# Grouped-query attention: V blocks loaded in two halves, other loads moved, and one set of Q transposes put later

## The chip, the core and the metric

The kernel runs on one core of a Trainium2 chip. A core has five engines that work side by side, each through its own list of instructions in order: TensorE (PE; matmuls, and a part for weight loads, PEld), VectorE (DVE), ScalarE (ACT), GpSimd (POOL) and SyncE (SP). Sixteen DMA engines move data between device memory and the core's SBUF. A DMA is issued by an engine's list, here SP's, POOL's or ACT's, and runs by itself from then on; an issue on POOL takes POOL's time. Matmuls write to PSUM, which PE, DVE and ACT reach.

The metric is the time on the device of one execution, in microseconds (us). It is the median of several executions; one more execution was recorded by the profiler.

## The reference

Q is (8, 512, 32, 64): batch, sequence, heads, dimension. K and V have 8 heads, each shared by four heads of Q. All are float32.

```python
scale = 1.0 / np.sqrt(dim)
scores = np.einsum('bhqd,bhkd->bhqk', Q, K_expanded) * scale
weights = np.exp(scores - np.max(scores, axis=-1, keepdims=True))
weights = weights / (np.sum(weights, axis=-1, keepdims=True) + 1e-10)
output = np.einsum('bhqk,bhkd->bhqd', weights, V_expanded)
return output.transpose(0, 2, 1, 3).astype(np.float32)
```

## The kernel before, in words

**Blocks, units and jobs.** The eight batch entries are the blocks 0 to 7. The work is cut into 64 jobs; a job `j` is one K/V head of one block with its four Q heads (two pairs), so block `b` has jobs 8b to 8b+7, and two jobs make a unit `u`. A job computes sixteen 128 x 512 pieces of scores (two pairs, four quarters of the keys, two heads), takes their exponentials, multiplies by V (with a column of ones behind V, so that the sums of the weights come out of the same products), and divides. No maximum is subtracted; `check_sums` and `check_v` gather evidence that this was safe, and a general path behind the fast one would run if it wasn't.

**Two ways to an exponential.** Most of a job's scores go two pieces at a time through ACT (`act_tile`, line 300; seven tiles in a job, numbered 0 to 6). Two or three pieces of each job go another way: DVE turns the scores into an integer `u` (`exp_d`, line 317), takes low bits `f` of it (line 334), POOL makes `g` of `f` (line 339) and `w` of `g` and `f` (line 345), and DVE adds `u` and `w` into the weights `pt` (`exp_d4`, line 358). The sum for job j is made in the loop step of job j+1, just ahead of job j+1's own `f`. So the chain goes round from POOL to DVE to POOL: `w` of one job, sum, `f`, `g`, `w` of the next.

**Kinds of jobs.** With `WIDE` and `ALONE` (lines 41 to 44) there are three: wide jobs give three pieces to DVE and POOL; narrow jobs (2, 8, 14, 20, ... 62) give two; and the wide job just ahead of a narrow one (7, 13, 19, 25, ...), called lone job here, has its `g` made by DVE instead of POOL, behind the first step of its last normalisation. Six jobs, from a narrow one to the next, make a round.

**The order of the work** is written out by hand: the loop at line 574 issues, for each job, the loads listed for it in `LOADS`, the K transposes listed in `KEYS`, the scores of this job, the products of the job before (`pv`, line 386, on PE), the normalisation of the job before (`norm`, lines 418 and 425, on DVE) and the transposes of a Q that will be used two jobs later (`trans_q`: eight transposes on PE, line 219, into a bank of PSUM, and one copy out by DVE, line 224). Waits between engines are put in by the language's bookkeeping of who wrote and read which tile. Where that bookkeeping would order two instructions that touch different banks of one tile, the kernel takes the order out by hand with `apart`, which tells it so; `trans_q` has an argument `other` for that.

**Loads.** All loads of Q, K and V in the loop are issued by POOL, at the head of the job's step, that is behind the `w` of the job before and ahead of the job's own `g`. `load_q` brings half a block of Q, `load_k` and `load_v` a block of K or V. V is held in two buffers, `vt[b % 2]`, four quarters of 128 keys each; V's block b overwrites block b-2, so it waits for the last product with that one, which is in the step of job 8(b-1). V rows lie 65 elements apart (the column of ones between), so a load of V writes 128 x 32 separate runs of 64 elements; a load of K writes 128 long runs, a load of Q 512. `check_v` (line 242) reads one quarter of a V block in each of four jobs listed in `CHECKS`; `check_sums` (line 399, three reductions) comes in the jobs of `SUMS`: 14, 20, 26, 38, 44, 50 and 62, narrow jobs all.

**K** is transposed by DMAs on SP's list (`dma_k`), which also stores the results; three result buffers are in turn.

**The start.** The first three jobs run by a branch of their own (`if j < 3`). In job 2 two sets of Q transposes are made instead of one, for jobs 3 and 4, into the two banks of one PSUM tile, one behind the other, between ACT tiles 3 and 4; Q for job 4 is loaded in job 1.

Of the kernel before, what the change touches and what calls it, by code (L numbers as in the profile page):

```python
# [70 lines left out]
def fast_path(ctx, tc, Q, K, V, out, flag, ident):  # L71
    nc = tc.nc
    B, S, H, D = Q.shape
    KV = K.shape[2]
    HPG = H // KV
    SC = S // 128
# [31 lines left out]
    vt = [const_pool.tile([128, SC, KV, D + 1], BF16, name=f"v{j}") for j in range(2)]  # L108
# [14 lines left out]

    def load_v(b, lo=0):
        to = vt[b % 2][:, :, lo:, 0:D]
        of = V[b, :, lo:, :].rearrange("(p sc) g d -> p sc g d", p=128)
        if lo:
            for sc in range(SC):
                nc.gpsimd.dma_start(out=to[:, sc], in_=of[:, sc])  # L129
        else:  # L130
            nc.gpsimd.dma_start(  # L131
                out=to.rearrange("p sc g d -> p (sc g) d"),
                in_=of.rearrange("p sc g d -> p (sc g) d"),
            )

# [15 lines left out]
    def d_tile():  # L151
        return d_pool.tile([128, 2, S], FP32, name="d_ps")
# [113 lines left out]
    SUMS = dict(zip((14, 20, 26, 38, 44, 50, 62), range(B - 1)))  # L266
    KEYS = dict(zip((4, 10, 17, 28, 33, 41, 52), range(1, B)))

    def in_jobs(load, first, jobs):
        for n, j in enumerate(jobs):  # L270
            LOADS.setdefault(j, []).append((load, first + n))

    LOADS = {1: [(load_q, 1, 0, 2 * HPG), (load_q, 1, 2 * HPG, 4 * HPG)]}
    in_jobs(load_k, 1, [3, 8, 15, 22, 30, 39, 46])
    in_jobs(load_q, 2, [3, 5, 9, 12, 16, 21, 23, 28, 33, 35, 40, 45, 47, 52])
    in_jobs(load_v, 1, [7, 13, 19, 25, 37, 43, 49])

# [16 lines left out]
    def act_tile(j, n):  # L294
        group = act_tiles(j)[n]
        i, kc, lo = group[0]
        ps = s_tile()
        for _, _, m in group:
            scores(j, ps[:, m, :], i, kc, m)
        return nc.scalar.activation(  # L300
            out=jobs[j]["pt"][:, i, kc, lo:, :], in_=ps[:, lo:, :], func=EXP, scale=scale
        )
# [203 lines left out]
    load_v_head(0, 1)  # L506
    load_v(0, 2)
    nc.gpsimd.memset(ones, 1.0)
# [65 lines left out]
    for j in range(1, NJOB - 1):  # L574
# [12 lines left out]
        def transposes(bank, beside=None):  # L587
            ahead = (j + 1,) if j < 2 else (3, 4) if j == 2 else (j + 2,)
            return [
                trans_q(to, bank[:, n, :], other=beside)[1]  # L590
                for n, to in enumerate(ahead) if to < NJOB
            ]

# [7 lines left out]
        if j < 3:  # L601
# [25 lines left out]
        elif taken(j) < 3:  # L627
# [8 lines left out]
            act_tile(j, 4)  # L636
            reads = transposes(d_tile()) if j + 2 < NJOB else []
            exp_d4(last)
            for read in reads:
                read()  # L640
# [8 lines left out]
        elif not ALONE(j):  # L649
# [15 lines left out]
            if after:  # L665
                act_tile(j, 6)
            reads = transposes(bank, beside)
            if not after:
                act_tile(j, 6)
            exp_d4(last)  # L670
            exp_d2(j)
            for read in reads:
                read()
            pv(last, 1, cut, 32)
            norm(last, 1)
        else:
# [11 lines left out]
            act_tile(j, 5)  # L688
            reads = transposes(bank, beside)
# [4 lines left out]
            for read in reads:  # L694
                read()
            open_job(j + 1)
# [149 lines left out]
```

## Time and profile before

| | |
|---|---|
| median of three executions | 406.32 us (405.81 to 406.45) |
| profiled execution, its own time | 405.98 us |
| its span, first to last instruction | 404.2 us |
| granted TensorE clock | 0.999 |
| ACT busy | 394.1 us, 97% |
| DVE busy | 369.6 us, 91% |
| PE busy | 362.4 us, 90% |
| POOL busy | 294.8 us, 73% |
| whole V loads in the loop, issue on POOL | 7 of 1765 ns |

A page of the profile gives busy times by engine and by group of instructions (line, engine, operation, what is written from what, shapes, count, busy us, mean ns, idle time before them and what ended it). Behind it the trace can be asked for the instructions of one engine in order of time, and for the busy time of every engine in chosen stretches of the span. A long busy share doesn't say that an engine is the bound in every stretch; what an engine waited for, and when, does. Instructions on ACT and DVE overlap a little where one follows the other at once, so the mean duration of an ACT tile (1118 ns) is longer than the step from one to the next.

### The profile page before, as it was taken

The numbers are of one execution on the slowest core, as the hardware profiler recorded it, in microseconds if no ns is written. First come the engines' busy times: TensorE is split into PE (matmuls) and PEld (weight loads), VectorE is DVE, ScalarE is ACT, GpSimd is POOL, SyncE is SP. The second block draws the span as 40 slices with busy tenths as digits, with TensorE's granted clock in tenths as the row PEclk, the third lists the DMA queues.
The fourth block names the chain that finished last, engine by engine and source line by source line (L and its number), as shares of the span: only waits on it lengthen the run. The fifth ranks groups of instructions, "written<-read, shape, count | busy, mean of one in ns | idle before, by whom it ended". The sixth has DMA issues, their size and how long they took to land.

```text
span 404.2 us, 13018 instructions
## 1 busy us (share of the span) xinstructions
PE 362.4 (90%) x5670; PEld 223.9 (55%) x5670; DVE 369.6 (91%) x645; ACT 394.1 (97%) x454; POOL 294.8 (73%) x173
## 2 busy tenths in 40 slices
PE   7999889998998998899999989988999899899885
PEld 3555556555554655555555555555555555555554
DVE  4779999999999999999989899999999999898896
ACT  6999999999999999999999999999999999999995
POOL 9848787696786687777767786876887676756853
PEclk9999999999999999999999999999999999999999
DMA  9999899989697997989719798699895968222216
GB/s 148 144 198 198 183 255 216 153 186 193 150 216 189 172 206 155 157 158 186 234 66 181 126 291 160 102 203 185 205 208 164 137 108 227 108 106 105 76 40 205
DMA packets 82893, 67.73 MB, mean 168 GB/s; under 512 B 52752, under 2 KB 57872, under 8 KB 82832
## 3 DMA queue, kind: packets, MB, share of 16 engines
q0 software_dynamic: 45072, 24.91, 49.2%
q1 hardware_dynamic: 36688, 41.49, 35.0%
q8 instruction: 45, 0.74, 0.8%
q10 hardware_dynamic: 1072, 0.46, 0.4%
q14 instruction: 16, 0.13, 0.1%
HBM read 50.33 MB, written 33.55 MB: 208 GB/s over the span
## 4 chain that ended last, share of the span: by engine, by line
POOL 28%; PE 27%; DVE 20%; ACT 19%; issue 3%; DMA 2%; ACTq 0%; POOLq 0%; DVEq 0%
ACT pt L300 19%; POOL w L345 17%; PE pv L386 13%; PE s_ps L282 10%; POOL g L339 8%; DVE pt L358 8%; DVE f L334 5%; PE d_ps L219 3%; DVE o_sb L425 3%; DMA q_nat<-in_Q_dram 2%; DVE u L317 2%; DVE qt L224 1%; POOL v L129 1%; DVE inv L418 1%; DVE g L339 1%
## 5 line engine op out<-in xcount | busy, mean ns | idle before, releaser
L300 ACT ACTIVATE pt<-s_ps 128x1024 f16<-128x1024 f32 x397 | 377.3, 1118 | 2.0 <-PE s_ps L282 0.7
L345 POOL TENSOR_TENSOR w<-g,f 128x1536 bf16<-128x1536 bf16 (+1 forms) x63 | 182.3, 2894 | 25.6 <-DVE g L339 21.3
L386 PEld LDWEIGHTS <-pt 128*128 128x128 f16 x4096 | 140.5, 98 | 69.2 <-DVE o_sb L425 35.6
L386 PE MATMUL pv<-v,pt 128*128 128x65 bf16 x4032 | 170.1, 195 | 7.1 <-DVE o_sb L425 5.5
L282 PE MATMUL s_ps<-qt,kt 64*128 64x512 bf16 x742 | 145.1, 384 | 21.1 <-ACT pt L300 17.7
L339 POOL TENSOR_SCALAR g<-f 128x1536 bf16<-128x1536 int16 (+1 forms) x52 | 71.1, 1368 | 76.3 <-DVE f L334 60.1
L317 DVE TENSOR_SCALAR u<-d_ps 128x1024 int16<-128x1024 f32 (+1 forms) x114 | 111.9, 981 | 2.1 <-PE d_ps L282 1.8
L282 PEld LDWEIGHTS <-kt 64*128 64x128 bf16 x960 | 50.0, 93 | 88.0 <-issue 62.2
L425 DVE TENSOR_TENSOR o_sb<-pv,inv 128x512 f32<-128x512 f32 x112 | 77.3, 691 | 3.7 <-DVE inv L418 0.2
L358 DVE TENSOR_TENSOR pt<-u,w 128x1536 uint16<-128x1536 int16 (+1 forms) x64 | 57.4, 897 | 3.1
L282 PE MATMUL d_ps<-qt,kt 64*128 64x512 bf16 x218 | 42.1, 377 | 4.9 <-DVE qt L224 4.3
L224 DVE COPY qt<-d_ps 128x1024 bf16<-128x1024 bf16 x62 | 42.4, 685 | 0.3
L219 PE MATMUL d_ps<-ident,q_nat 128*128 128x128 bf16 x496 | 38.2, 220 | 0.4 <-DMA q_nat<-in_Q_dram 0.4
L334 DVE TENSOR_SCALAR f<-u 128x1536 int16<-128x1536 int16 (+1 forms) x64 | 37.6, 588 | 0.0
L310 ACT ACTIVATE pt<-d_ps 128x512 f16<-128x512 f32 x50 | 35.0, 701 | 0.0
L418 DVE RECIPROCAL inv<-pv 128x8 f32<-128x8 f32 x112 | 22.7, 203 | 12.3 <-PE pv L386 11.9
L219 PEld LDWEIGHTS <-q_nat 128*128 128x128 bf16 x508 | 29.0, 98 | 8.2 <-issue 7.5
L242 DVE TENSOR_REDUCE okv<-v 128x1 f32<-128x512 bf16 x32 | 21.6, 675 | 0.0
L146 POOL DMA_DIRECT2D q_nat<-in_Q_dram x19 | 15.5, 817 | 0.1
L282 PE MATMUL s_ps<-qt,kt_first 64*128 64x512 bf16 x54 | 10.3, 382 | 2.5 <-ACT pt L300 1.8
L131 POOL DMA_DIRECT2D v<-in_V_dram x7 | 12.4, 1765 | 0.0
L425 DVE TENSOR_TENSOR o_sb<-pv,inv_last 128x512 f32<-128x512 f32 x14 | 9.7, 691 | 0.4
(61 smaller groups left out, 60.5 us busy)
## 6 DMA issues: line engine op xcount, KB each, us to landing
out_dram<-o_sb SPq DMA_DIRECT2D x31, 1024.0 KB, 5.9
q_nat<-in_Q_dram POOLq DMA_DIRECT2D x14, 1024.0 KB, 10.5
k_nat<-in_K_dram POOLq DMA_DIRECT2D x7, 512.0 KB, 5.3
kt<-kt SPq DMA_DIRECT2D x14, 256.0 KB, 5.4
v<-in_V_dram POOLq DMA_DIRECT2D x7, 512.0 KB, 8.3
q_nat<-in_Q_dram POOLq DMA_DIRECT2D x3, 512.0 KB, 7.9
out_dram<-o_sb SPq DMA_DIRECT2D x3, 256.0 KB, 2.4
kt<-k_nat SPq DMA_TRANSPOSE x32, 6.3
```

The costliest lines, as they stand in the source:

```text
L219: nc.tensor.transpose(ps[:, i, sc, :], qn[u // 2][:, sc, h:h + 2, :], ident),
L224: return done, lambda: apart(nc.vector.tensor_copy(out=qt[u][:, g, lo:hi, :], in_=ps[:, lo:hi, :, :].rearrange("p i sc c -> p i (sc c)")), ...
L282: return nc.tensor.matmul(ps, keys[64 * m:64 * m + 64, g if u == 0 else g ^ m, kc * 128:(kc + 1) * 128], qt[u][64 * m:64 * m + 64, g, i, : ...
L300: return nc.scalar.activation(out=jobs[j]["pt"][:, i, kc, lo:, :], in_=ps[:, lo:, :], func=EXP, scale=scale)
L310: left = nc.scalar.activation(out=st["pt"][:, i, kc, m:, :], in_=ps[:, m:, :], func=EXP, scale=scale)
L317: return nc.vector.tensor_scalar(out=out, in0=in_, scalar1=A_U, scalar2=B_U, op0=ALU.mult, op1=ALU.add)
L334: nc.vector.tensor_single_scalar(out=st["f"], in_=st["u"], scalar=1023, op=ALU.bitwise_and)
L339: (nc.vector if odd else engine).tensor_scalar(out=st["g"], in0=st["f"], scalar1=-EXP_F1, scalar2=EXP_K * 2.0 ** (24 * by_bits), op0=ALU.a ...
L345: engine.tensor_tensor(out=st["w"], in0=st["g"], in1=st["f"].bitcast(FP16) if by_bits else st["f"], op=ALU.mult,)
L358: nc.vector.tensor_tensor(out=st["pt"][:, DPAIR, :, :, :].rearrange("p kc m q -> p (kc m) q")[:, d_block(j):d_block(j) + n, :].bitcast(U16 ...
L386: nc.tensor.matmul(st["pv"][i][:, m, qc, :], st["pt"][:, i, kc, m, qc * 128:(qc + 1) * 128], vt[b % 2][:, kc, 2 * gp + g, :], start=(n < 2 ...
L425: nc.vector.tensor_tensor(out=osb[u][:, :, h:h + 2, :].rearrange("p qc m d -> p m qc d"), in0=sums[:, :, :, 0:D], in1=inv[:, :, :, None].t ...
```

## The change

**V.** `load_v` takes two of the four quarters at a time. Block 1 is still loaded whole, in job 7. Blocks 2 to 7 come in two issues each, in jobs 9 and 14, 20 and 21, 26 and 27, 33 and 38, 44 and 45, 50 and 51: narrow jobs or the ones behind these. Before, they came whole in jobs 13, 19, 25, 37, 43 and 49, which are lone jobs. The opening's V load is the same four issues under another name.

**Other loads.** Q loads move from jobs 9, 21, 33 and 45 to 10, 22, 34 and 46, K loads from 22 and 46 to 24 and 48. The K transposes of block 5 on SP move from job 33 to job 35.

**Job 2.** The second set of Q transposes, for job 4, and its copy go behind ACT tile 4 and the first eleven products of the second pair. The rest of the edits turn lists of one into single values.

```diff
-    def load_v(b, lo=0):
-        to = vt[b % 2][:, :, lo:, 0:D]
-        of = V[b, :, lo:, :].rearrange("(p sc) g d -> p sc g d", p=128)
-        if lo:
-            for sc in range(SC):
-                nc.gpsimd.dma_start(out=to[:, sc], in_=of[:, sc])
-        else:
-            nc.gpsimd.dma_start(
-                out=to.rearrange("p sc g d -> p (sc g) d"),
-                in_=of.rearrange("p sc g d -> p (sc g) d"),
-            )
+    def load_v(b, lo=0, hi=SC):
+        nc.gpsimd.dma_start(
+            out=vt[b % 2][:, lo:hi, :, 0:D].rearrange("p sc g d -> p (sc g) d"),
+            in_=V[b].rearrange("(p sc) g d -> p sc g d", p=128)[:, lo:hi].rearrange(
+                "p sc g d -> p (sc g) d"
+            ),
+        )
+
+    def first_v(lo):
+        of = V[0, :, lo:, :].rearrange("(p sc) g d -> p sc g d", p=128)
+        for sc in range(SC):
+            nc.gpsimd.dma_start(out=vt[0][:, sc, lo:, 0:D], in_=of[:, sc])
...
-    KEYS = dict(zip((4, 10, 17, 28, 33, 41, 52), range(1, B)))
+    KEYS = dict(zip((4, 10, 17, 28, 35, 41, 52), range(1, B)))
...
-    in_jobs(load_k, 1, [3, 8, 15, 22, 30, 39, 46])
-    in_jobs(load_q, 2, [3, 5, 9, 12, 16, 21, 23, 28, 33, 35, 40, 45, 47, 52])
-    in_jobs(load_v, 1, [7, 13, 19, 25, 37, 43, 49])
+    in_jobs(load_k, 1, [3, 8, 15, 24, 30, 39, 48])
+    in_jobs(load_q, 2, [3, 5, 10, 12, 16, 22, 23, 28, 34, 35, 40, 46, 47, 52])
+    in_jobs(load_v, 1, [7])
+    for b, at in enumerate(((9, 14), (20, 21), (26, 27), (33, 38), (44, 45), (50, 51)), 2):
+        for n, j in enumerate(at):
+            LOADS.setdefault(j, []).append((load_v, b, n * SC // 2, (n + 1) * SC // 2))
...
-    load_v(0, 2)
+    first_v(2)
...
         def transposes(bank, beside=None):
-            ahead = (j + 1,) if j < 2 else (3, 4) if j == 2 else (j + 2,)
-            return [
-                trans_q(to, bank[:, n, :], other=beside)[1]
-                for n, to in enumerate(ahead) if to < NJOB
-            ]
+            return trans_q(j + (1 if j < 3 else 2), bank[:, 0, :], other=beside)[1]
...
             bank = d_tile()
-            reads = transposes(bank)
-            if j == 1:
-                reads.append(first_k(1, 1, bank[:, 1, :])[1])
+            read = transposes(bank)
+            beside = first_k(1, 1, bank[:, 1, :])[1] if j == 1 else None
             exp_d4(last)
             exp_d2(j)
-            for read in reads:
-                read()
+            read()
+            if beside:
+                beside()
             act_tile(j, 4)
             pv(last, 1, 0, 11)
+            if j == 2:
+                trans_q(4, bank[:, 1, :])[1]()
             act_tile(j, 5)
...
```

More of the change, by code (lines that the diff above doesn't have):

```diff
@@ L636, in fast_path @@
             act_tile(j, 4)
-            reads = transposes(d_tile()) if j + 2 < NJOB else []
+            read = transposes(d_tile()) if j + 2 < NJOB else None
             exp_d4(last)
-            for read in reads:
+            if read:
                 read()
@@ L666, in fast_path @@
                 act_tile(j, 6)
-            reads = transposes(bank, beside)
+            read = transposes(bank, beside)
             if not after:
@@ L671, in fast_path @@
             exp_d2(j)
-            for read in reads:
-                read()
+            read()
             pv(last, 1, cut, 32)
@@ L688, in fast_path @@
             act_tile(j, 5)
-            reads = transposes(bank, beside)
+            read = transposes(bank, beside)
             act_tile(j, 6)
@@ L693, in fast_path @@
             rest = exp_d2(j)
-            for read in reads:
-                read()
+            read()
             open_job(j + 1)
```

## The prediction

> **What bounds the kernel now.** I read the page's first parts, then stretches of the span cut at the starts of narrow jobs, then the order of instructions on single engines. The page first:
>
> ```profile
> span 404.2 us, 13018 instructions
> PE 362.4 (90%) x5670; PEld 223.9 (55%) x5670; DVE 369.6 (91%) x645; ACT 394.1 (97%) x454; POOL 294.8 (73%) x173
> ```
>
> ACT is 97% busy, so a gain can only be time in which ACT runs late. Busy stretches of six jobs, each from the first exp of a narrow job to that of the next, show where (columns: stretch, us, then busy us and instructions of PE, weight loads, DVE, ACT, POOL; clock; DMA). The clock is 1.00 in all:
>
> ```profile
> 55.85:92.32 36.47, 33.57 (x534) 20.64 (x530) 34.59 (x59) 36.47 (x43) 28.31 (x15) 1.00 1.03 176
> 129.08:165.82 36.74, 33.40 (x534) 20.65 (x530) 35.47 (x62) 36.60 (x44) 28.27 (x15) 1.00 0.97 199
> 165.82:202.57 36.75, 33.40 (x534) 20.64 (x530) 35.46 (x63) 36.61 (x43) 25.83 (x13) 1.00 0.94 173
> 202.57:238.91 36.34, 33.33 (x533) 20.75 (x530) 32.03 (x54) 36.34 (x43) 27.73 (x14) 1.00 0.77 168
> 349.78:386.12 36.34, 33.31 (x533) 20.73 (x530) 31.98 (x55) 36.34 (x44) 24.53 (x11) 1.00 0.24 89
> ```
>
> The two stretches of 36.34 us are those whose lone job just ahead (31, 55) issues no V load. Two with V loads take 36.74 and 36.75, the first 36.47; the other V stretches are like these two or longer. The narrow jobs alone (14 to 20 and so on; here 20, 32, 62 and 8):
>
> ```profile
> 129.08:135.93 6.85, 5.89 (x96) 3.65 (x93) 6.78 (x16) 6.71 (x8) 3.20 (x2) 1.00 1.65 212
> 202.57:208.90 6.33, 5.96 (x96) 3.76 (x93) 5.66 (x12) 6.33 (x8) 3.28 (x2) 1.00 0.00 0
> 386.12:392.45 6.33, 5.55 (x89) 3.40 (x86) 6.13 (x15) 6.33 (x9) 3.45 (x2) 1.00 0.01 3
> 55.85:62.38 6.53, 6.07 (x96) 3.65 (x93) 5.91 (x13) 6.53 (x8) 3.75 (x3) 1.00 1.46 111
> ```
>
> Job 20 has a V load ahead and the three reductions of `check_sums` (16 DVE instructions): 6.85. Job 62 has the reductions and no V load: 6.33, as job 32 with neither. Job 8 has a V load and no reductions: 6.53. So V is needed for the loss, and the loss is 0.52 us where both meet. What V does there, on POOL and DVE around jobs 13 to 16, and DVE in job 31, which has no V load (instructions in order of time: start us, us, engine, line, operation; in brackets the idle time before it and what ended it):
>
> ```profile
> 90.54 1.77 POOL L131 DMA_DIRECT2D v<-in_V_dram  x1
> 93.90 3.08 POOL L345 TENSOR_TENSOR w<-g,f 128x1536 bf16<-128x1536 bf16 x1 [1.58 <-DVE g L339]
> 102.27 0.62 POOL L118 DMA_DIRECT2D k_nat<-in_K_dram  x1
> ...
> 90.63 0.96 DVE L358 TENSOR_TENSOR pt<-u,w 128x1536 uint16<-128x1536 int16 x1
> 91.50 1.17 DVE L334 TENSOR_SCALAR f<-u 128x1536 int16<-128x1536 int16 x1
> 98.49 0.42 DVE L334 TENSOR_SCALAR f<-u 128x1024 int16<-128x1024 int16 x1
> 103.46 0.55 DVE L334 TENSOR_SCALAR f<-u 128x1536 int16<-128x1536 int16 x1
> 106.57 0.67 DVE L242 TENSOR_REDUCE okv<-v 128x1 f32<-128x512 bf16 x1
> ...
> 200.88 0.96 DVE L358 TENSOR_TENSOR pt<-u,w 128x1536 uint16<-128x1536 int16 x1
> 201.76 0.56 DVE L334 TENSOR_SCALAR f<-u 128x1536 int16<-128x1536 int16 x1
> ```
>
> The V issue occupies POOL for 1.77 us (90.54 to 92.31). The DVE step `f` that begins at 91.50 beside it takes 1.17 us instead of 0.55 or 0.56: its work ran from 92.12 (92.67 less 0.55), 0.19 us before the issue's recorded end. The sum `pt<-u,w` beside the same issue is not slowed (0.96 both times). So `f` waits while POOL issues, and `g`, `w` and the next narrow job come 0.61 us late.
>
> **The change, part by part.** *V halves.* A half writes half the runs of 64 elements: 128 x 16 = 2048. Issue times per load, by runs: 4096 for a whole V, 768 for the opening's quarter loads, 512 for a full Q, 128 for a full K:
>
> ```profile
> L131 POOL DMA_DIRECT2D v<-in_V_dram x7 | 12.4, 1765 | 0.0
> L129 POOL DMA_DIRECT2D v<-in_V_dram x4 | 3.4, 891 | 0.0
> L146 POOL DMA_DIRECT2D q_nat<-in_Q_dram x19 | 15.5, 817 | 0.1
> L118 POOL DMA_DIRECT2D k_nat<-in_K_dram x9 | 5.8, 644 | 0.0
> ```
>
> A line from 768 to 4096 gives 891 + 1280 x 0.263 ns = 1.23 us, one from 128 gives 1.19; I take 1.2, with ends 0.64 and 1.77. Six whole loads (10.6 us of POOL) become twelve halves (14.4 us). Where they go:
> In narrow job 14 POOL is free from 96.98 (end of `w`), and its next step, `g`, needs `f`, which starts at 98.49 behind the sum and the `qt` copy. A half from 96.9 ends at 98.1: it meets no `f` and holds up no `g`. Cost 0; without that cover, 1.2.
> In the job behind POOL comes to its loads at 102.27 (here K's); a half would run to 103.47, let `f` go at 103.28 by the 0.19 above, and `f` is due at 103.46: cost 0, with 0.18 to spare. At the upper end (1.77) it would let go at 103.85, and `f` would be 0.39 late: 6 x 0.39 = 2.3 us. Jobs 9 and 33 wait also for the last reader of the old V; PE finishes job 7's last products at 61.97 and POOL gets to its load at 65.48:
>
> ```profile
> 61.30 0.67 PE L386 MATMUL pv<-v,pt 128*128 128x65 bf16 x16
> 65.48 0.82 POOL L146 DMA_DIRECT2D q_nat<-in_Q_dram  x1
> 73.54 1.47 POOL L339 TENSOR_SCALAR g<-f 128x1536 bf16<-128x1536 int16 x1 [1.55 <-DVE f L334]
> L131 POOL DMA_DIRECT2D v<-in_V_dram x7: 1762/1762/1771, 53.8 to 311.0; - x7
> DMA to landing us min/median/max: 7.5/8.3/10.7
> ```
>
> That leaves 3.5 us, so nothing queued behind on POOL (`g`, `w`) waits. What is gained: jobs 13, 19, 25, 37, 43 and 49 lose their V load, job 7 keeps it. A plain stretch takes 36.75 (mean of the two shown) against 36.34: 0.41 each (0.52 in the narrow job, 0.11 given back later, since POOL's loop g, w, `pt`, `f` is then next to bind), 6 x 0.41 = 2.46 us. What makes some V stretches longer still I leave as it is.
>
> The Trainium skill, "SBUF — State Buffer", section "Who interferes with whom", says that a DVE instruction in a two-port mode and GpSimd lock each other out for the whole instruction. By it `f` would start only at 92.31, at 1.2 us the job behind would lose 6 x 0.01, and at 1.77 it would lose 6 x 0.58 = 3.5 instead of 2.3; the measured start, 92.12, is kinder, and I go by it.
>
> *Q and K moved.* Four Q loads go one job later, two K loads two jobs: each stands alone in a wide job, where POOL waits 1.55 us for `f` (row at 73.54) and the issue takes 0.82 or 0.64. Cost 0; uncovered, 0.8 each. Nobody needs them for four jobs (24 us at 36.34 / 6 each). The transposes of K block 5 on SP start two jobs later; stores behind them have three buffers. Cost 0. The opening's four V loads are the same.
>
> *Third job.* Rows of PE, ACT and DVE in job 2, and of DVE in job 1:
>
> ```profile
> 20.98 0.62 PE L219 MATMUL d_ps<-ident,q_nat 128*128 128x128 bf16 x8
> 21.96 0.62 PE L219 MATMUL d_ps<-ident,q_nat 128*128 128x128 bf16 x8 [0.36 <-DMA q_nat<-in_Q_dram]
> 22.51 0.39 PE L282 MATMUL s_ps<-qt,kt_first 64*128 64x512 bf16 x2
> ...
> 22.95 6.52 ACT L300 ACTIVATE pt<-s_ps 128x1024 f16<-128x1024 f32 x7 [0.52 <-PE s_ps L282]
> 29.29 0.67 ACT L310 ACTIVATE pt<-d_ps 128x512 f16<-128x512 f32 x1
> ...
> 15.78 0.42 DVE L334 TENSOR_SCALAR f<-u 128x1024 int16<-128x1024 int16 x1
> 16.11 0.69 DVE L224 COPY qt<-d_ps 128x1024 bf16<-128x1024 bf16 x1
> 22.21 0.42 DVE L334 TENSOR_SCALAR f<-u 128x1024 int16<-128x1024 int16 x1
> 22.62 1.29 DVE L224 COPY qt<-d_ps 128x1024 bf16<-128x1024 bf16 x2
> ```
>
> Now PE stands 0.36 us before the second set, whose Q lands at 21.96, and ACT idles 0.52. ACT's step per tile is (29.29 - 22.95) / 7 = 0.91; tiles that follow closely overlap, so about 0.2 more is lost: the fifth tile (number 4 from 0) could begin at 22.23. With the second set moved, the scores of tile 4 run at 21.53 and that 0.72 us is won. But the moved set writes the second half of a two-bank tile after the copy out of its first half has been put into the program. The kernel declares such pairs free of each other wherever it wants them so (`apart`, "the two are in different banks of one tile"), and the new call passes no `other`. So I take it that PE must now wait for the first copy. The rows hint at such whole-tile waits: in job 2 the first copy starts 0.41 after `f`, just when the second set ends (22.58), in job 1 0.33 after. In the new order the copy runs from 22.54 to 23.23, PE transposes from about 23.28 to 23.83 (0.55 to the next start, as 21.96 to 22.51), and the scores of tile 5 end at 24.22, so that ACT has them at 24.27 (0.44 after the PE start, as 22.51 to 22.95). Before, tile 5 began at 22.95 + 0.91 = 23.86. Net loss 0.41, bounds -0.57 (no wait: scores of tile 5 from 22.85, ACT at 23.29) and +0.41. What is queued on PE behind the wait (scores of tiles 5 and 6, the products between, job 3) shifts with it, and ACT, the bound, has nothing to give it back with. The copy of the moved set is needed only in job 4.
>
> The Trainium skill, "PSUM — Partial Sum Buffer", section "PSUM bank collisions raise a hardware error", has accesses of two engines to different banks run clean. By it no wait is needed between the copy and the moved set, and the sum here would be -0.57; no run here shows which the program does.
>
> *Sum.* -2.46 + 0.41 = -2.05 us. The profiled execution took 405.98 us (span 404.2 and 1.8 around it), 0.34 below the median of 406.32, so 403.9 profiled and 404.3 as a median.
>
> **Rivals.** *No wait on the copy.* Speaks for it: two different banks. Against it: the missing declaration. -2.46 - 0.57 gives 403.3.
> *The gain isn't V's.* The two stretches of 36.34 us lack not only V but also the reductions and the checks of V (DVE 32.0 against 35.5 us busy). Were DVE late for those, only job 8's share would come back: 36.47 - 36.34 = 0.13 each, 0.8 in all: 405.9. Against it: job 62. Or the halves take `f` with them in the job behind, at the upper end of their issue: -2.05 + 2.3 gives 406.6.
> *Slower: V lands late for its check.* DVE reads the first quarter of a V block in jobs 22, 28, 46 and 52, two jobs after its half is issued instead of three after the whole. By job 14 (issue from 96.9) and job 16 (check at 106.57) that leaves 9.7 us. A whole V lands in 7.5 to 10.7 us; a half should take less. Were each a microsecond and a half over that, `f` and everything behind DVE's wait would slip four times: 4 x 1.5 - 2.05 = +4.0, 410.3. It outweighs the gain from 9.7 + 2.05/4 = 10.2 us on.
>
> **How the numbers follow.** Forecast 0.60 (its own range 403.5 to 405.0); no wait on the copy 0.13; gain not V's, or lost behind the narrow jobs, 0.16; V late 0.06; small things I don't see 0.05. About 0.2% (0.8 us, so 405.5 to 407.1) is what a measurement here can tell from no change. Faster: 0.60 + 0.13 + 0.05 from the third case + 0.01; same: 0.11 of the third and 0.02; slower: 0.06 and 0.02. The range 402.9 to 405.9 takes in the no-wait case with a margin and the 405.9 of the third.
>
> **What would show it.** Every 1536-wide `f` at 0.55, but job 7's; V issues of 1.2 us, twelve; stretches of 36.3 from job 14 on, narrow jobs at 6.33; in job 2 a PE wait of about a microsecond for DVE's `qt` copy and ACT idle of about 0.9 at tile 5. Wrong if `f` is long in jobs 9, 15 or 21, if DVE waits for V in job 22, or if ACT doesn't stop in job 2.

## The result and the profile after

The changed kernel took 404.48 us (median of 14 executions, 404.03 to 405.72), the kernel before 406.02 us measured beside it. The ratio is 0.9966, with a 95% interval of 0.9957 to 0.9975: 1.0 to 1.7 us faster. One of the 14 executions of the kernel before took 488.24 us and is left out of the ratio. The profiled execution of the changed kernel took 404.53 us at a clock of 0.999. Line numbers move by four: ACT's tiles are now line 304, `f` is 338, `g` 343, `w` 349, the copy `qt` 225.

The first lines of the changed kernel's page:

```profile
span 402.8 us, 13022 instructions
PE 362.8 (90%) x5670; PEld 225.2 (56%) x5670; DVE 366.4 (91%) x645; ACT 392.6 (97%) x454; POOL 298.6 (74%) x179
```

Three of the stretches of six jobs, which answer to those of before (columns as there: stretch, us, busy us and instructions of PE, weight loads, DVE, ACT, POOL; clock; DMA):

```profile
129.67:166.04 36.37, 33.34 (x534) 20.86 (x531) 34.90 (x62) 36.37 (x44) 28.91 (x16) 1.00 0.92 189
166.04:202.41 36.37, 33.36 (x535) 20.85 (x532) 34.90 (x62) 36.37 (x44) 28.16 (x15) 1.00 1.07 182
202.41:238.77 36.36, 33.33 (x534) 20.85 (x531) 32.04 (x55) 36.36 (x43) 27.20 (x14) 1.00 0.79 133
```

The two stretches that took 36.74 and 36.75 us now take 36.37, hardly more than the one that never had a V load ahead of it (36.36). From the start of job 8 to that of job 62 it was 386.12 - 55.85 = 330.27 us before and is 384.65 - 56.88 = 327.77 now: 2.50 us less. Job by job, the six narrow jobs behind the old V loads take 3.03 us less in sum, and the other jobs 0.54 more, of it 0.18 in job 22 alone. The longest stretches, from jobs 38 and 50, went from 37.09 and 37.03 us to 36.57 and 36.64, so they gained as well but did not come to 36.3. Narrow jobs 20 and 8, and job 2:

```profile
129.67:136.04 6.37, 5.99 (x98) 3.88 (x95) 6.24 (x15) 6.37 (x9) 4.46 (x3) 1.00 0.40 128
56.88:63.43 6.55, 6.08 (x96) 3.66 (x93) 5.92 (x13) 6.55 (x9) 3.76 (x3) 1.00 1.52 141
19.25:26.73 7.48, 6.25 (x96) 3.96 (x96) 5.10 (x10) 6.56 (x8) 4.21 (x4) 1.00 1.00 136
```

Job 20 went from 6.85 to 6.37, beside 6.36 and 6.32 for jobs 32 and 62; job 8, behind the one whole load that is left, stays at 6.55. Job 2 takes 7.48 us. V's issue in job 21 on POOL, and on DVE `f` of job 13, which lost its load, and of job 21:

```profile
139.03 1.22 POOL L125 DMA_DIRECT2D v<-in_V_dram  x1
...
92.54 0.55 DVE L338 TENSOR_SCALAR f<-u 128x1536 int16<-128x1536 int16 x1
140.35 0.55 DVE L338 TENSOR_SCALAR f<-u 128x1536 int16<-128x1536 int16 x1
```

The twelve halves take POOL 1.22 to 1.24 us each, and `f` is 0.55 or 0.56 us in every wide job but 7. In job 2, on PE, ACT and DVE:

```profile
23.94 0.61 PE L220 MATMUL d_ps<-ident,q_nat 128*128 128x128 bf16 x8 [0.89 <-DVE qt L225]
...
24.91 5.61 ACT L304 ACTIVATE pt<-s_ps 128x1024 f16<-128x1024 f32 x6 [0.92 <-PE s_ps L286]
...
23.20 0.68 DVE L225 COPY qt<-d_ps 128x1024 bf16<-128x1024 bf16 x1
```

PE stands 0.89 us for DVE's first copy, and ACT stands 0.92 us for the scores behind it. The span shrank by 1.4 us (404.2 to 402.8), though, and not by the forecast's 2.05. The rest is in the opening, which both kernels share. The first exponentials on ACT in the two profiled executions, before and then after:

```profile
5.47 1.09 ACT L546 ACTIVATE pt<-s_ps 128x512 f16<-128x512 f32 x2 [0.59 <-PE s_ps L282]
```

```profile
6.12 1.08 ACT L550 ACTIVATE pt<-s_ps 128x512 f16<-128x512 f32 x2 [0.93 <-PE s_ps L286]
```

ACT begins 0.65 us later. So -2.50 (jobs 8 to 61) + 0.41 (job 2, 7.48 against 7.07) + 0.65 = -1.44.

### The profile page after: what moved, and what is told of

Same layout as the page of the kernel before. It is cut to its first block, busy times and chain, and to the rows that moved or that the text cites. A ratio compares the mean times of both kernels' runs of the same rounds, so it can differ in the third digit from the quotient of the medians.

```text
span 402.8 us, 13022 instructions
## 1 busy us (share of the span) xinstructions
PE 362.8 (90%) x5670; PEld 225.2 (56%) x5670; DVE 366.4 (91%) x645; ACT 392.6 (97%) x454; POOL 298.6 (74%) x179
## 4 chain that ended last, share of the span: by engine, by line
ACT 44%; PE 33%; DVE 11%; POOL 8%; issue 2%; ACTq 0%; DVEq 0%; POOLq 0%
ACT pt L304 42%; PE pv L390 15%; PE s_ps L286 13%; POOL w L349 5%; DVE pt L362 4%; PE d_ps L220 4%; POOL g L343 3%; DVE f L338 2%; ACT pt L314 2%; DVE u L321 2%; DVE o_sb L429 1%; DVE qt L225 1%; PE s_ps L518 1%; DVE inv L422 1%; ACT pt L550 0%
## 5 line engine op out<-in xcount | busy, mean ns | idle before, releaser
L286 PEld LDWEIGHTS <-kt 64*128 64x128 bf16 x960 | 51.1, 93 | 90.4 <-issue 65.1
L314 ACT ACTIVATE pt<-d_ps 128x512 f16<-128x512 f32 x50 | 37.9, 758 | 0.0
L338 DVE TENSOR_SCALAR f<-u 128x1536 int16<-128x1536 int16 (+1 forms) x64 | 33.9, 530 | 0.0
L125 POOL DMA_DIRECT2D v<-in_V_dram x13 | 16.5, 1267 | 0.0
```

The costliest lines, as they stand in the source:

```text
L286: return nc.tensor.matmul(ps, keys[64 * m:64 * m + 64, g if u == 0 else g ^ m, kc * 128:(kc + 1) * 128], qt[u][64 * m:64 * m + 64, g, i, : ...
L314: left = nc.scalar.activation(out=st["pt"][:, i, kc, m:, :], in_=ps[:, m:, :], func=EXP, scale=scale)
L338: nc.vector.tensor_single_scalar(out=st["f"], in_=st["u"], scalar=1023, op=ALU.bitwise_and)
```

## The experiments

Each version was measured beside executions of the kernel before on the same chip, whose median was between 406.06 and 406.27 us. Times are medians; a ratio is to that kernel, with its 95% interval in brackets. Times of versions that ran on different chips compare best by their ratios.

**V and the other loads alone.** Job 2 in its old order:

```diff
         def transposes(bank, beside=None):
-            return trans_q(j + (1 if j < 3 else 2), bank[:, 0, :], other=beside)[1]
+            ahead = (j + 1,) if j < 2 else (3, 4) if j == 2 else (j + 2,)
+            return [
+                trans_q(to, bank[:, n, :], other=beside)[1]
+                for n, to in enumerate(ahead) if to < NJOB
+            ]
...
-            if j == 2:
-                trans_q(4, bank[:, 1, :])[1]()
```

> The changed kernel with the third job's order put back as it was before: V, Q, K and the K transposes alone. Theory (the prediction's sum): the loss of 0.41 us in job 2 goes away and nothing else changes. Job 2 (first ACT tile of job 2 to that of job 3) takes 7.07 us instead of 7.48, the stretches from job 14 on 36.3, the time 0.4 us below the changed kernel's, 404.1. Rival (the set is moved because ACT gives the 0.41 back later, or the opening's first loads matter more): the time is the changed kernel's within 0.2 us.

404.13 us (403.52 to 405.34), ratio 0.9955 (0.9942 to 0.9967). Job 2 and the stretch of job 20 in its profile:

```profile
19.16:25.70 6.54, 6.19 (x96) 4.07 (x96) 5.08 (x10) 6.54 (x8) 3.27 (x3) 1.00 0.86 158
128.67:165.04 36.37, 33.35 (x534) 20.86 (x531) 34.91 (x62) 36.37 (x44) 28.94 (x16) 1.00 0.91 185
```

The time is as expected, and the stretches are those of the changed kernel: from job 8 to job 62 it gains the same 2.50 us. So the loads carry the whole gain. Job 2 is not as expected: it takes 6.54 us, not 7.07. Its opening was late too (job 1 begins at 12.76 us, in the first profile of before at 12.20), and then the Q for job 4 had arrived before PE came to it: nothing of the 0.36 us wait is left.

**Job 2 alone.** The loads of before, with the new order in job 2:

```diff
-            beside = first_k(1, 1, bank[:, 1, :])[1] if j == 1 else trans_q(4, bank[:, 1, :])[1] if j == 2 else None
+            beside = first_k(1, 1, bank[:, 1, :])[1] if j == 1 else None
...
             pv(last, 1, 0, 11)
+            if j == 2:
+                trans_q(4, bank[:, 1, :])[1]()
```

> The kernel before with the third job's new order alone. Theory: PE waits about 0.9 us for DVE's copy ahead of the moved set, ACT stands about 0.9 us ahead of its fifth tile, job 2 takes 7.48 us instead of 7.07, and the time is 0.4 us above that of the kernel before. Rival: later jobs give it back, and the time is that of before.

407.04 us, ratio 1.0015 (1.0006 to 1.0023): slower by 0.2 to 0.9 us. Its PE in job 2:

```profile
23.85 0.61 PE L220 MATMUL d_ps<-ident,q_nat 128*128 128x128 bf16 x8 [0.89 <-DVE qt L225]
```

The same wait as in the changed kernel, ACT's 0.92 us behind it, and job 2 at 7.47 us. Nothing later gives it back.

**The wait declared away.** One thing more in the changed kernel: its transposes into the second bank are declared free of the copy out of the first.

```diff
-            read()
+            copied = read()
...
-                trans_q(4, bank[:, 1, :])[1]()
+                done, read = trans_q(4, bank[:, 1, :])
+                for this in done:
+                    apart(this, copied)
+                read()
```

> The changed kernel with one line more: the moved set's transposes are declared free of the first copy, which reads the other bank of the tile. Theory (PE's wait is one of bookkeeping, not of the chip): the wait of 0.89 us is gone, PE transposes right behind the products, ACT stands at most 0.1 us ahead of tile 5, job 2 takes 6.5 us (7.48 less 0.98), and the time is 1.0 us below the changed kernel's: 403.5. Rival 1 (PE's writes and DVE's reads in two banks of one tile disturb each other): transposes or copy get longer by some tenths, and less than 1.0 is won. Rival 2 (the next thing is late: PE's scores have too little lead): ACT stands at tile 6 or in job 3 instead, and less than half is won.

403.88 us (403.23 to 404.50), ratio 0.9941 (0.9928 to 0.9954). PE, ACT and DVE in job 2:

```profile
23.09 0.61 PE L220 MATMUL d_ps<-ident,q_nat 128*128 128x128 bf16 x8
...
20.37 9.32 ACT L304 ACTIVATE pt<-s_ps 128x1024 f16<-128x1024 f32 x10
...
23.41 1.28 DVE L225 COPY qt<-d_ps 128x1024 bf16<-128x1024 bf16 x2
```

PE doesn't wait, ACT runs ten tiles without a gap, and job 2 takes 6.42 us instead of 7.48: 1.06 won where 0.98 was expected. PE now writes the second bank (from 23.09) while DVE reads the first (from 23.41), and neither is longer for it: 0.61 us as before, and two copies in 1.28. So the wait was one of bookkeeping. That is what the Trainium skill, "PSUM — Partial Sum Buffer", section "PSUM bank collisions raise a hardware error", has for accesses to different banks, and this trace agrees. By the ratios (0.9941 and 0.9966) the time fell by 1.0 us, as expected; by the medians alone, 403.88 and 404.48, by 0.6. The profiled execution has the latest opening of all (job 1 begins at 13.06).

**Whole V, in the narrow jobs.**

```diff
-    for b, at in enumerate(((9, 14), (20, 21), (26, 27), (33, 38), (44, 45), (50, 51)), 2):
-        for n, j in enumerate(at):
-            LOADS.setdefault(j, []).append((load_v, b, n * SC // 2, (n + 1) * SC // 2))
+    in_jobs(load_v, 2, [14, 20, 26, 38, 44, 50])
```

> The changed kernel with V blocks 2 to 7 not in halves: whole loads of 1.77 us, in the narrow jobs 14, 20, 26, 38, 44 and 50 alone. It tells whether the halves or the place bring the gain. Theory (only an f that falls beside an issue waits): the issue from 96.9 to 98.7 would let f go at 98.48, when it is due at 98.49, so f is 0.42 us in the narrow jobs and 0.55 in those behind, the stretches stay at 36.3 to 36.4, and the time is the changed kernel's within 0.3 us. Rival 1 (the length of an issue counts wherever it stands): each of six rounds loses 0.3 to 0.4 us, the time is 2 us above. Rival 2 (V late for its check): the whole block lands 7.5 to 10.7 us behind its issue and is read 9.7 us behind it, so DVE waits for the load in some of jobs 16, 22, 28, 40, 46 and 52, up to 1 us each.

409.48 us, ratio 1.0103 (1.0078 to 1.0127). The stretch from job 20, then jobs 39 and 40, and two of the waits from 250 to 256 us (engine, line, what for: us, times, longest):

```profile
129.26:165.63 36.37, 33.35 (x534) 20.86 (x531) 34.92 (x62) 36.37 (x44) 28.28 (x15) 1.00 0.87 169
...
245.00:254.37 9.37, 5.92 (x89) 3.67 (x89) 5.40 (x10) 6.10 (x9) 7.57 (x5) 0.94 1.98 196
254.37:261.92 7.55, 7.55 (x89) 4.44 (x87) 5.79 (x10) 6.30 (x7) 2.13 (x3) 0.63 1.07 285
```

```profile
PEld L284 <- DMA kt<-kt: 3.3, 1, 3.3
PE s_ps L284 <- DMA kt<-kt: 3.0, 1, 3.0
```

The time is that of none of the three theories. The stretch from job 20 is as fast as with halves, as the first had it, so the place brings the gain. The loss is in one place that none had named: jobs 39 and 40 take 9.37 and 7.55 us instead of 5.91 and 5.90. In job 39 PE waits 3.0 us for K of block 5. Job 40 waits for no load, but the granted clock, 1.00 until then, is 0.50 from 253.5 to 260 us, and sixteen products of `pv` take 1.06 us instead of 0.66: the slower clock behind the wait is a third of the loss. The mean granted clock is 0.990 or 0.991 in all six executions, which speaks for the same in all of them.

The move of the K transposes from job 33 to job 35 is behind the wait. On SP's list the last step of these, before, changed and here:

```profile
225.59 1.12 SPq L202 DMA_DIRECT2D kt<-kt  x2
```

```profile
241.98 1.12 SPq L203 DMA_DIRECT2D kt<-kt  x2
```

```profile
244.19 1.83 SPq L203 DMA_DIRECT2D kt<-kt  x2
```

It is issued at 225.59 us in the kernel before and at 241.98 in the changed one, for job 40 that begins at 251.3. Here it comes at 244.19, beside the whole V of job 38 (issued from 242.37), and is late.

**The same with the K transposes back in job 33.**

```diff
-    KEYS = dict(zip((4, 10, 17, 28, 35, 41, 52), range(1, B)))
+    KEYS = dict(zip((4, 10, 17, 28, 33, 41, 52), range(1, B)))
```

> The changed kernel with V blocks 2 to 7 whole in the narrow jobs 14, 20, 26, 38, 44 and 50, and the K transposes of block 5 back in job 33 instead of 35. With the transposes in job 35, whole loads stood 4.7 us at jobs 39 to 41, where PE waited for kt of block 5 while V's packets of job 38 were under way; every other round was as fast as with halves. Theory (that one collision is the whole difference, and the place of the loads, not the halving, brings the gain): the wait for kt is gone, jobs 39 and 40 take 5.9 us each, and the time is the changed kernel's within 0.3 us (404.2 to 404.8). Rival (whole loads cost in the rounds for another reason, or kt is late again): the time stays above 406.

404.49 us (404.12 to 405.30), ratio 0.9950 (0.9937 to 0.9964): the changed kernel's time. The stretch from job 20 and job 40, and then, in order of time, DVE in job 40:

```profile
129.59:165.96 36.37, 33.35 (x535) 20.86 (x531) 34.91 (x62) 36.37 (x44) 28.29 (x15) 1.00 0.93 190
251.24:257.83 6.59, 5.23 (x88) 3.28 (x86) 5.60 (x10) 6.18 (x9) 4.91 (x4) 1.00 0.76 152
```

```profile
253.75 0.69 DVE L243 TENSOR_REDUCE okv<-v 128x1 f32<-128x512 bf16 x1 [0.96 <-DMA v<-in_V_dram]
```

The wait for K is gone, the mean clock is 0.997 to 0.999, and job 39 takes 5.91 us. So it is not the halving of V that gains, but taking it out of the lone jobs. A whole load two jobs ahead of its check does come late once: DVE waits 0.96 us for V in job 40, which takes 6.59 instead of 5.91.

**The reductions moved, V left where it was.** The kernel before with:

```diff
-    SUMS = dict(zip((14, 20, 26, 38, 44, 50, 62), range(B - 1)))
+    SUMS = dict(zip((15, 21, 27, 39, 45, 51, 62), range(B - 1)))
```

> The kernel before with the three reductions of the sums taken out of the narrow jobs 14, 20, 26, 38, 44 and 50 and put one job later; V stays whole in the lone jobs. Theory (the 0.52 us are lost where f's delay by V and the reductions meet): f stays at 1.17 us in the lone jobs, the narrow jobs take 6.53 us, as job 8 with V and no reductions, instead of 6.87, so 0.34 each, 2.0 us in all, less what the reductions cost the jobs behind (0 to 0.1 each): the time 1.4 to 2.0 us below that of before. Rival (V's delay alone costs the narrow job, and the reductions only happen to stand there): narrow jobs stay at 6.8 to 6.9 and the time is that of before.

406.53 us, ratio 1.0006 (0.9997 to 1.0015). Job 20, and then, in order of time, `f` of job 19 on DVE:

```profile
129.68:136.54 6.86, 5.91 (x96) 3.66 (x93) 6.24 (x13) 6.73 (x9) 3.21 (x2) 1.00 1.59 192
```

```profile
128.87 1.16 DVE L334 TENSOR_SCALAR f<-u 128x1536 int16<-128x1536 int16 x1
```

The theory fell: job 20 has 13 DVE instructions instead of 16 and still takes 6.86 us. The reductions have no part in the loss. What is left is V's delay of `f`, and the next experiment measures it.

**V in doses in the lone jobs.** The changed kernel, K transposes in job 33, and

```diff
+    for b, lone, cut in ((2, 13, 2), (3, 19, 3), (4, 25, 1), (5, 37, 4), (6, 43, 2), (7, 49, 3)):
+        LOADS.setdefault(lone, []).append((load_v, b, 0, cut))
+        if cut < SC:
+            LOADS.setdefault(lone + 1, []).append((load_v, b, cut, SC))
```

> The changed kernel with the first part of each V block back in the lone job and the rest in the narrow job behind it, in doses: block 2 a half in job 13, block 3 three quarters in 19, block 4 one quarter in 25, block 5 all of it in 37, block 6 a half in 43, block 7 three quarters in 49; the K transposes of block 5 in job 33. It measures how the narrow job's loss goes with f's delay in the lone job. Issues take 0.96, 1.22, 1.49 and 1.77 us for one to four quarters, f is due 0.97 us behind the issue's start. Theory (f is let go 0.19 us before the recorded end, and the narrow job loses f's delay less about 0.1 us): f in the lone jobs 0.55, 0.61, 0.88 and 1.16 us, by dose; the narrow jobs take, against the changed kernel's 6.32, 6.37, 6.37, 6.64, 6.33, 6.38: job 14 the same, job 20 0.23 more (6.6), job 26 the same, job 38 0.5 more (7.13), job 44 the same, job 50 0.23 more (6.6). Rival 1 (f waits for the whole issue): f 0.80 for a half and 1.07 for three quarters, the narrow jobs behind a half 0.15 more and behind three quarters 0.4 more. Rival 2 (the loss comes with V's packets or its landing, not with f): all six narrow jobs lose 0.5, or none does.

404.98 us in one execution. `f` on DVE and V's issue on POOL beside it, in job 13 (half), 19 (three quarters) and 37 (whole), and then the narrow jobs 14, 20 and 38:

```profile
92.23 0.63 DVE L339 TENSOR_SCALAR f<-u 128x1536 int16<-128x1536 int16 x1
91.26 1.24 POOL L125 DMA_DIRECT2D v<-in_V_dram  x1
128.56 0.89 DVE L339 TENSOR_SCALAR f<-u 128x1536 int16<-128x1536 int16 x1
127.59 1.50 POOL L125 DMA_DIRECT2D v<-in_V_dram  x1
237.75 1.16 DVE L339 TENSOR_SCALAR f<-u 128x1536 int16<-128x1536 int16 x1
236.79 1.77 POOL L125 DMA_DIRECT2D v<-in_V_dram  x1
```

```profile
93.04:99.37 6.33, 5.92 (x96) 3.65 (x93) 6.26 (x15) 6.33 (x8) 4.35 (x3) 1.00 1.14 207
129.37:135.96 6.59, 6.12 (x98) 3.69 (x94) 6.52 (x16) 6.59 (x8) 4.08 (x3) 1.00 1.12 76
238.57:245.70 7.13, 6.18 (x99) 3.77 (x95) 7.06 (x16) 6.84 (x8) 3.47 (x2) 1.00 1.17 78
```

All six as the theory has them. `f` is 0.08 us late beside a half, 0.34 beside three quarters, 0 beside a quarter (job 25), 0.61 beside a whole load; jobs 43 and 49 repeat the half and the three quarters with 0.62 and 0.90. The narrow jobs behind, 14, 20, 26, 38, 44 and 50, take 6.33, 6.59, 6.33, 7.13, 6.33 and 6.62 against the changed kernel's 6.32, 6.37, 6.37, 6.64, 6.33 and 6.38: they lose nothing beside a half or a quarter, 0.22 and 0.24 behind three quarters, 0.49 behind a whole load, the delay less about 0.1. The end of the issue less the start of `f`'s own 0.55 us of work is 92.50 - 92.31, 129.09 - 128.90 and 238.56 - 238.36: 0.19, 0.19 and 0.20.

**Three quarters behind the narrow jobs.**

```diff
+    for b, big, small, lo in (
+        (2, 9, 14, 0), (3, 21, 20, 1), (4, 27, 26, 1), (5, 33, 38, 0), (6, 45, 44, 1), (7, 51, 50, 1),
+    ):
+        LOADS.setdefault(big, []).append((load_v, b, lo, lo + 3))
+        LOADS.setdefault(small, []).append((load_v, b, *((0, 1) if lo else (3, 4))))
```

> The changed kernel with V in three quarters and one quarter instead of two halves: the three quarters in the jobs behind the narrow ones (9, 21, 27, 33, 45, 51), one quarter in 14, 20, 26, 38, 44, 50. It measures the prediction's 0.18 us to spare in the job behind. By the line through the issue times (1.22 us for 2048 runs, 1.77 for 4096) three quarters take 1.50 us. Theory (f is let go 0.19 us before the recorded end of an issue): f is let go 0.12 us after it is due in jobs 21, 27, 45 and 51 and takes 0.67 us instead of 0.55; jobs 9 and 33 have spare and stay at 0.55; the time is 0 to 0.5 us above the changed kernel's. Rival (f waits for the whole issue): f takes 0.85 to 0.9. Rival 2 (a load beside f costs nothing at all in a wide job): 0.55 everywhere.

408.04 us in one execution. No `f` is late in jobs 21, 27, 33, 45 and 51 (all 0.55 or 0.56 us beside issues of 1.48 to 1.49): with the lone jobs no longer late, `f` is due 1.31 us behind the issue's start (139.31 to 140.62 in job 21), not the 1.19 of the kernel before. The time is lost elsewhere. Job 9 takes 6.44 us instead of 5.91, where PE stands 0.8 us for V, and jobs 37 and 38 take 8.77 and 7.01 instead of 5.91 and 6.64. There, PE, and what the DMA queues moved from 228 to 240 us (packets, MB, share of 16 engines):

```profile
236.62 0.29 PE L220 MATMUL d_ps<-ident,q_nat 128*128 128x128 bf16 x2
239.35 0.49 PE L220 MATMUL d_ps<-ident,q_nat 128*128 128x128 bf16 x6 [2.45 <-issue]
```

```profile
q8 instruction: 1, 0.02, 4.1%
```

PE stops between the second and the third of eight transposes of one Q, a Q loaded in job 28, and the trace has nothing that it waits for. One packet of the instruction queue took 4.1% of 16 x 12 us, that is 7.9 us; in the changed kernel two packets take 1.5%. Behind the stop the granted clock is 0.50 from 240.4 to 243.6 us.

**The same with the K transposes in job 33.** The edit to `KEYS` shown above.

> The version with three quarters of V and one quarter, and the K transposes of block 5 back in job 33. With the transposes in job 35 it stood 3.6 us in jobs 37 and 38: PE had done two of eight Q transposes and stood 2.45 us with nothing that the trace names to wait for, and one packet of the instruction queue, begun at 229.9, had taken 7.9 us instead of about 1, beside the packets of the K transposes (229 to 245 us) and of two Q loads. Theory (PE stood for its own code, which came late behind the transposes' packets): with the transposes in job 33 these are done by about 222 us, the code packet near 230 takes 0.9 to 1.8 us, jobs 37 and 38 take 5.9 and 6.6, and the time is 404 to 405. Rival (V's three quarters in job 33, 3072 runs, are the cause, wherever the K transposes stand): PE stands again for 1 us or more between 220 and 250.

404.55 us in one execution. Job 37, and the instruction queue from 228 to 240 us:

```profile
232.86:238.78 5.92, 5.28 (x87) 3.37 (x87) 5.22 (x10) 5.92 (x9) 4.11 (x2) 1.00 1.06 291
```

```profile
q8 instruction: 2, 0.03, 0.9%
```

The stall is gone (job 38 takes 6.62), with V as it was; job 9 takes 5.92 as well, though nothing was changed there, so its 0.53 us came by chance. This is one execution of each version, and the account of the stall rests on it.

**The kernel before, once more.**

> The kernel before, unchanged, for one more look at its opening. In the first profile ACT began job 1 at 12.20 us and job 3 at 25.67; in the changed kernel and four others with the same opening job 1 began at 12.44 to 13.06. Theory (the opening's loads come late by chance, and in the old order PE's wait for the Q of job 4 takes that up): whatever the start of job 1, job 3 begins at 25.6 to 25.8, and a later start shows in a shorter wait of PE for that Q. Rival (the change itself delays the opening): job 1 begins at 12.2 again.

406.19 us in one execution. Job 1 began at 12.80 us, job 2 took 6.54 us and job 3 began at 25.75 (25.67 in the first profile). The first exponentials:

```profile
6.08 1.08 ACT L546 ACTIVATE pt<-s_ps 128x512 f16<-128x512 f32 x2 [0.93 <-PE s_ps L282]
```

So the late opening is chance and not the change. The version with the reductions moved, which has the old order too, shows the limits of the theory: there the Q came late as well, PE waited 0.61 us, job 2 took 7.33 and job 3 began at 26.28.

**V of block 1 early.** The declaration, and:

```diff
-    in_jobs(load_v, 1, [7])
+    in_jobs(load_v, 1, [3])
```

> The changed kernel with the moved transposes declared free of the first copy, and with V of block 1 in job 3 instead of job 7: a version meant to be faster than both. In job 3 POOL stood 3.6 us idle ahead of g, so the issue of 1.77 us meets no f. Theory: f in job 7 takes 0.55 instead of 1.00 us, job 8 takes 6.32 instead of 6.53, everything else stands as with the declaration alone, and the time is 0.2 us below that version's 403.9: 403.7. Rival (the load so early delays the Q and K loads around it): ACT stands somewhere in jobs 4 to 7, and the time is above 403.9.

406.09 us (403.99 to 408.36), ratio 0.9993 (0.9969 to 1.0017). The time is the rival's, but only a part of the loss is. `f` in job 7 takes 0.55 us and job 8 6.44 instead of 6.53, not the 6.32 of the theory. V landed 22.2 us behind its issue (8.7 in the changed kernel), the last step of K of block 1 was issued at 48.99 us instead of 44.25, and PE waited for it in job 7, which took 6.91 us instead of 5.92:

```profile
56.35 0.39 PE L286 MATMUL s_ps<-qt,kt 64*128 64x512 bf16 x1 [0.84 <-DMA kt<-kt]
```

The profiled execution's span is 2.6 us longer than that of the declaration alone. Job 7 is 1.0 us of it. Another 2.0 us are lost far behind, 1.0 each in jobs 37 and 39, with the K transposes in job 35: in job 37 PE stopped again between the second and the third transpose, for 1.23 us, and in job 39 it waited for K of block 5. The clock stayed at 1.00 there. Why the executions spread over 4.4 us is open; the slowest, of 407.0 to 408.4 us, have mean clocks of 0.990 to 0.996.

**A version that beats both.** The declaration, the K transposes in job 33, and V of block 1 in two halves in jobs 6 and 7:

```diff
-    in_jobs(load_v, 1, [7])
-    for b, at in enumerate(((9, 14), (20, 21), (26, 27), (33, 38), (44, 45), (50, 51)), 2):
+    for b, at in enumerate(((6, 7), (9, 14), (20, 21), (26, 27), (33, 38), (44, 45), (50, 51)), 1):
```

> The version meant to be faster than both: the changed kernel with the moved transposes declared free of the first copy, the K transposes of block 5 back in job 33, and V of block 1 in two halves, in jobs 6 and 7. A half beside f in a wide or lone job delays it 0.07 to 0.13 us (measured: f 0.62 beside a half in jobs 13 and 43), which cost the narrow job nothing. Theory: f in job 7 takes 0.62 instead of 1.00 us, job 8 takes 6.33 instead of 6.53, job 2 takes 6.42, no wait for K or Q in jobs 37 to 41, and the time is 0.2 us below the 403.9 of the declaration alone: 403.7. Rival (V of block 1 in the middle of the first K transposes delays something, as V in job 3 did): jobs 7 or 8 take longer, and the time is above 404.

402.94 us (402.89 to 403.45), ratio 0.9926 (0.9912 to 0.9939), below the changed kernel's 0.9957 to 0.9975. Job 8 and job 2:

```profile
55.37:61.70 6.33, 5.95 (x96) 3.75 (x93) 5.60 (x12) 6.33 (x8) 3.86 (x3) 1.00 1.31 189
18.77:25.20 6.43, 6.11 (x96) 3.92 (x96) 5.00 (x10) 6.43 (x9) 3.17 (x3) 1.00 1.03 171
```

Job 8 gained the 0.2 us expected. The time fell by 0.9 against the declaration alone, and the two profiled executions, which took 402.89 and 403.88 us, tell of what: 0.20 is job 8, and 0.70 is the opening (job 1 begins at 12.36 us instead of 13.06), which is the same code in both; the other jobs are equal within 0.1. So 0.2 is gained and 0.7 is chance there. The K transposes gave nothing in these two profiles, but they may steady the time: its executions lie within 0.6 us, those of the four versions that differ from it least and have these in job 35 (the changed one, V alone, the declaration, V early) within 1.3 to 4.4; but whole loads with them in job 33 spread over 1.2 too.

## Why the prediction was right

**V halves, 2.46 us.** Measured 2.50, and by the parts that were forecast: 0.52 in each narrow job and 0.11 given back behind it make 3.12 and 0.66 in six rounds; 3.03 and 0.54 came. The issue of a half was put at 1.2 us and is 1.22 to 1.24; all wide `f` but job 7's are 0.55 or 0.56; the stretches shown came to 36.37 instead of 36.34. That `f` waits while POOL issues, and is let go 0.19 us before the recorded end, held at three lengths of issue. The Trainium skill, "SBUF — State Buffer", section "Who interferes with whom", has the later one shut out for the whole instruction; here `f` was let go 0.19 or 0.20 us before the recorded end each time.

**"The loss is 0.52 us where both meet."** This step was wrong, though the sum didn't feel it: without the reductions the narrow job lost the same. What set job 8 apart was not their absence but the size of `f`'s delay: 1.00 us in job 7, 0.45 late, against 0.61, and there the sum `pt` came 0.20 us behind `w` instead of 0.03. The loss there was the delay less 0.25 us, against less 0.1 in the doses; that the late sum is the reason is argued, not shown. The row that would have told it stands in the prediction: job 62, with the reductions and no V, at 6.33. It was read as "V is needed", when with job 8 it leaves the choice open between "both" and "V alone, by its dose".

**"With 0.18 to spare" in the job behind.** It is more: half issues there end at 140.25 in job 21, `f` could go at 140.06 and goes at 140.35, 0.29 to spare. The rows of before had it 0.12 us too early, because the POOL loop itself was late there.

**The halves.** The prediction took the halving and the moving together. The runs separate them: whole loads in the narrow jobs give the same stretches. What the halves buy is landing: whole, V came 0.96 us late for its check once. This is the mechanism of the prediction's slower rival, at a load twice the size. Halves are no guard against it either: the prediction expected them to land faster than the 7.5 to 10.7 us of a whole load, and the twelve took 4.8 to 12.5 us, with a median of 5.8. The 12.5 us were in job 38, with the K transposes in job 35; the block's quarter that is checked first had come in job 33.

**"Q and K moved: cost 0."** The changed kernel's profile has no wait for them. But what the K transposes need is time to land, and the prediction should have named it: their last step went from 225.59 to 241.98 us. Of the six versions that were profiled with the transposes in job 35, three lost 2 to 5 us in jobs 37 to 40 to late K or to PE's stop; of the eight profiles with job 33 none did, and in the two that were run again with job 33 as the only edit the loss was gone.

**Third job, +0.41.** PE's wait (0.89, "about a microsecond"), ACT's idle time (0.92, "about 0.9") and job 2's 7.48 us came as worked out, and the run with the declaration showed the wait to be one of bookkeeping. The term was mis-sized all the same: it took the 7.07 us of one execution for the old order's. That order took 6.54 us in two profiles, 7.07 and 7.33 in others, by when the Q of job 4 arrived, and the new one 7.47 or 7.48 always. So the cost is 0.15 to 0.94 us; measured alone, 0.2 to 0.9.

**What the sum left out.** -2.05 was forecast, -1.54 measured in medians (1.0 to 1.7 by the ratio). Part is the dearer job 2. The new order also lets the opening's chance through to the end: job 3 then begins 13.9 us behind job 1 in every profile without the declaration, where with the old order it was 12.9 to 13.7, less where the opening was late and the Q of job 4 had come meanwhile. Whether the rest, in executions that were not profiled, is the K transposes stays open. The granted clock speaks against a stall with a halved clock: the two profiles that had one have a mean of 0.991 and 0.993, the changed kernel's executions have 0.997 to 1.000. V alone gained 2.5 us in its profiled execution (span 401.7 against 404.2), the fastest of its six, and 1.3 to 2.4 by the interval of them all.

## What to carry to other kernels

Where a load's issue delays a step, find the place in the loop where no such step is due, and size the delay by dose (issue length less the time to the step); cutting the load is the second choice, worth it for its landing. A load or transpose that is moved by two jobs may cost nothing in the profile and still have spent the time that the next change needs: compare when its last piece is issued with when it is read. One profile gives a wait on a DMA as a number, when it is one draw of many; look at a second execution before it enters a sum. A wait of PE can cost more than its length, so look at the granted clock behind it. And when a tile has two banks and PE and DVE use different ones, a wait of PE on DVE is worth one declaration.

## What the runs showed of the hardware

**PE's code.** PE seems to have stood still for its own code. From the changed kernel's page:

```profile
q8 instruction: 45, 0.74, 0.7%
```

These are 45 packets of 16.4 KB. With the packets of the K transposes on the DMA engines one took 7.9 us, and PE stood 2.45 us in the midst of eight equal transposes; in the eight profiles with the transposes in job 33 no packet took over 2.9 us, and PE didn't stop there. That the packet was PE's code is inferred: at 237.8 us it ended and 1.55 us later PE went on. In the version with V early a packet of 2.3 us ended at 236.1, and PE went on 1.6 us later at the same place. With whole V in the narrow jobs one of 4.1 us ended at 233.3, about 3 us before PE came there, and PE didn't stop. The Trainium skill, "Runtime: NRT & Kernel Launch", section "Instruction fetch mechanics", has each engine's code brought in blocks of 16 KiB by a DMA queue of its own, at a cost "mostly hidden". The size agrees; hidden it was not here.

**PE's clock behind a stall.** After PE had stood for 3.04 us (whole V in the narrow jobs) and for 2.45 us (three quarters), the granted clock was 0.50 for 6.8 and 3.4 us, and sixteen products took 1.06 us in the first case, not 0.66. After stops of 0.89 us (job 2) and 1.23 us (V early) it stayed at 1.00. What decides between these cases, no run here shows.
